# Operations of five attention rounds moved ahead or behind in the order of a hybrid decoder layer

## The chip, the cores and the metric

The kernel runs on one core of a Trainium2 chip. The core's engines are called as in the profile: PE (TensorE, matrix products), ACT (ScalarE), DVE (VectorE), POOL (GpSimd), SP (SyncE, which here issues the weight loads). Each engine works through its own queue of instructions; semaphores hold an instruction until what it reads is there, or until the buffer that it writes is free. The metric is the device time of one execution in microseconds; the time of a kernel is the median of several executions.

## The reference, cut to what matters

The kernel computes one layer of a decoder in float32 for 512 tokens of width 1024. Two token mixers run side by side on the normalised input: NSA, a sparse attention of 8 heads in 2 key/value groups, and GLA, a gated linear attention in chunks. Memory cross-attention and a gated ConvFFN follow. The change touches the NSA part, whose core is

```python
s = s - slopes * dist
p_cmp = masked_softmax(s, dist >= 0)          # compressed keys: 31 of them
o_cmp = jnp.einsum('bhgqn,bnhd->bqhgd', p_cmp, v_cmp)
...
p_slc = masked_softmax(s, mask)               # selected blocks: with 8 blocks of 64, all keys up to the query
o_slc = jnp.einsum('bhgqk,bhqkd->bqhgd', p_slc, vg)
...
p_win = masked_softmax(s, mask)               # the window: at most 256 keys back
o_win = jnp.einsum('bhgqk,bkhd->bqhgd', p_win, vwb)
```

The three results are weighted by sigmoid gates and added.

## The kernel before

**Tiling.** Tokens are cut into four blocks of 128, features into tiles of 128. A float32 operand that must keep its precision is split into a high and a low part: ACT writes the high part (`wh`, `pth`, lines 140 and 165) and DVE the rest (`wl`, `ptl`, lines 141 and 166). A product of two such operands is three matmuls (lines 160 to 162, or 197 to 199). Weights arrive as `raw` tiles from SP's queue and are split on the way.

**Rounds.** The attention runs in eight rounds, one for each key/value group `kv` and token block `i`; round r is `kv*4 + i`. `nsa_scores` forms the scores of four heads in PSUM (PE, lines 581, 597 to 613), adds the mask and takes the row maximum (DVE, lines 583 to 585, 603, 615), exponentiates (ACT, line 631, eight a round, after DVE's `nm` of line 622), sums and takes the reciprocal (DVE, lines 627, 634, 635) and scales the probabilities by the gates (DVE line 639, ACT lines 641 and 643, POOL line 645). `nsa_values` takes the scaled probabilities in pieces of 128 keys: four transposes into a PSUM bank `pt` (PE, line 669), the split into `pth` and `ptl` (ACT, then DVE), and two products into the bank `o` (PE, line 663); at the end ACT and DVE add the two halves (lines 683, 688) and split the result. The loop turn of round r issues first the values of round r-1 (`nsa_values(*prev)`), then the scores of round r (`nsa_scores(kv, i)`), then `fill(...)`: matmuls of other work (`fill_ps_acc`, dense products of the GLA projections), so that PE has something to do. The values of round 7 come last, behind the loop.

**After the rounds** comes the GLA part. `dense_tok` (lines 197 to 199) makes the GLA values: 96 matmuls into four banks (`acc_533`, `acc_534`, `sc_535`, `sc_536`), which nothing holds up but weights and banks, so that the scheduler puts them between the pieces of rounds 5 to 7. Then `gla_att` (line 814), `gla_states` (line 769, 21 matmuls, then a chain of DVE operations, line 781) and further fillers, the first of which is `fill_ps_acc_583`.

**PSUM** has eight banks: two `acc`, three `sc`, two `pt`, one `o`.

**What sets the order.** The code is written round by round, and a scheduler of the framework puts each engine's instructions into a fixed order, by priorities that follow the place in the code; `tc.high_priority(offset=n)` shifts the priority of what is issued inside it by n places, ahead for n > 0 and behind for n < 0. An engine then keeps that order, whatever becomes ready first.

## Time and profile before

| | us |
|---|---|
| time before, median of three runs | 864.42 (863.22 to 865.28) |
| profiled execution, its own time | 862.94 |
| profiled execution, span from the first to the last instruction | 861.1 |
| PE busy in the span | 848.0 (98%) |
| DVE busy | 564.7 (66%) |
| ACT busy | 424.5 (49%) |
| POOL busy | 175.5 (20%) |

Times in views of the trace are microseconds from the start of the span. In a timeline, a row is a run of like instructions of one engine: its start, the time it took, the engine and line, the operation with its output and inputs (buffer numbers left out), the count, and in brackets how long the engine had stood idle before it and for whom. The durations of PE's rows overlap, since matmuls are pipelined; the distance between starts says how fast PE goes.

### The profile page before, as it was taken

The numbers are of one execution on the slowest core, as the hardware profiler recorded it, in microseconds if no ns is written. First come the engines' busy times: TensorE is split into PE (matmuls) and PEld (weight loads), VectorE is DVE, ScalarE is ACT, GpSimd is POOL, SyncE is SP. The second block draws the span as 40 slices with busy tenths as digits, with TensorE's granted clock in tenths as the row PEclk, the third lists the DMA queues.
The fourth block names the chain that finished last, engine by engine and source line by source line (L and its number), as shares of the span: only waits on it lengthen the run. The fifth ranks groups of instructions, "written<-read, shape, count | busy, mean of one in ns | idle before, by whom it ended". The sixth has DMA issues, their size and how long they took to land.

```text
span 861.1 us, 11067 instructions
## 1 busy us (share of the span) xinstructions
PE 848.0 (98%) x4172; PEld 707.6 (82%) x4172; DVE 564.7 (66%) x930; ACT 424.5 (49%) x742; POOL 175.5 (20%) x150
## 2 busy tenths in 40 slices
PE   9999999999999999999999999999999999999997
PEld 6988788777878888898888888888888888888996
DVE  7576998989979667454587759665433455656434
ACT  8466878787444455344455545433311233334321
POOL 2373354412000024203200412111100022121001
PEclk9999999999999999999999999999999999999999
DMA  8332210102221242254331132222222222222402
GB/s 293 120 127 98 74 50 25 49 25 74 74 77 58 86 147 98 97 173 144 127 120 49 56 116 99 99 98 97 98 98 98 98 99 98 97 98 78 143 25 99
DMA packets 26406, 83.58 MB, mean 97 GB/s; under 512 B 3056, under 2 KB 5104, under 8 KB 26352
## 3 DMA queue, kind: packets, MB, share of 16 engines
q1 hardware_dynamic: 26064, 82.58, 27.7%
q8 instruction: 33, 0.54, 0.2%
q10 hardware_dynamic: 288, 0.28, 0.1%
q14 instruction: 21, 0.17, 0.1%
HBM read 80.76 MB, written 2.10 MB: 96 GB/s over the span
## 4 chain that ended last, share of the span: by engine, by line
PE 89%; DVE 5%; ACT 4%; issue 1%; POOL 1%; DMA 0%; DVEq 0%; ACTq 0%; POOLq 0%
PE up_ps_sc L160 4%; PE up_ps_sc L162 4%; PE up_ps_sc L161 4%; PE fill_ps_acc L160 4%; PE fill_ps_acc L161 4%; PE fill_ps_acc L162 3%; PE up_ps_pt L160 3%; PE up_ps_pt L162 3%; PE up_ps_pt L161 3%; PE up_ps_acc L160 3%; PE up_ps_acc L162 3%; PE up_ps_acc L161 3%; PE nsa_ps_o L663 2%; PE nsa_ps_pt L669 2%; PE down_ps_sc L162 2%; PE down_ps_sc L160 2%
## 5 line engine op out<-in xcount | busy, mean ns | idle before, releaser
L1091 POOL TENSOR_TENSOR up_s<-up_s,up_s 128x512 f32<-128x512 f32 x22 | 40.2, 1827 | 253.6 <-ACT up_wh L140 201.8
L140 ACT ACTIVATE up_wh<-up_raw 128x1024 fp32r<-128x1024 f32 x40 | 42.4, 1061 | 56.5 <-PE up_ps_sc L161 29.7
L141 DVE TENSOR_TENSOR up_wl<-up_raw,up_wh 128x1024 fp32r<-128x1024 f32 x40 | 58.2, 1456 | 15.5 <-ACT up_wh L140 15.4
L160 PE MATMUL up_ps_sc<-xo_g,up_wh 128*128 128x512 f32 x124 | 48.3, 389 | 0.0
L162 PE MATMUL up_ps_sc<-xo_g,up_wl 128*128 128x512 f32 x124 | 48.3, 389 | 0.0
L161 PE MATMUL up_ps_sc<-xo_g,up_wh 128*128 128x512 f32 x124 | 48.2, 389 | 0.0
L160 PE MATMUL up_ps_pt<-xo_g,up_wh 128*128 128x512 f32 x104 | 40.5, 389 | 0.0
L162 PE MATMUL up_ps_pt<-xo_g,up_wl 128*128 128x512 f32 x104 | 40.5, 389 | 0.0
L161 PE MATMUL up_ps_pt<-xo_g,up_wh 128*128 128x512 f32 x104 | 40.5, 389 | 0.0
L160 PE MATMUL fill_ps_acc<-in_g,fill_wh 128*128 128x512 f32 x96 | 38.8, 404 | 0.8 <-DVE fill_t L548 0.8
L161 PE MATMUL fill_ps_acc<-in_g,fill_wh 128*128 128x512 f32 x96 | 38.6, 402 | 0.0
L162 PE MATMUL fill_ps_acc<-in_g,fill_wl 128*128 128x512 f32 x96 | 38.2, 398 | 0.0
L631 ACT ACTIVATE nsa_s<-nsa_s,nsa_nm 128x128 f32<-128x128 f32 (+3 forms) x64 | 34.2, 538 | 6.5 <-DVE nsa_nm L622 6.5
L160 PE MATMUL up_ps_acc<-xo_g,up_wh 128*128 128x512 f32 x88 | 34.2, 389 | 0.0
L161 PE MATMUL up_ps_acc<-xo_g,up_wh 128*128 128x512 f32 x88 | 34.2, 389 | 0.0
L162 PE MATMUL up_ps_acc<-xo_g,up_wl 128*128 128x512 f32 x88 | 34.2, 389 | 0.0
L1087 ACT ACTIVATE up_s<-up_s 128x512 f32<-128x512 f32 x22 | 13.8, 632 | 40.9 <-DVE up_s L1085 40.9
L140 ACT ACTIVATE down_wh<-down_raw 128x1024 fp32r<-128x1024 f32 x9 | 9.5, 1061 | 39.4 <-PE down_ps_sc L161 17.5
L165 ACT ACTIVATE nsa_pth<-nsa_ps_pt 128x512 fp32r<-128x512 f32 x38 | 21.9, 594 | 11.0 <-PE nsa_ps_pt L669 10.7
L162 PEld LDWEIGHTS up_ps_sc<-xo_g,up_wl 128*128 128x128 f32 x124 | 23.3, 188 | 4.9
L161 PEld LDWEIGHTS up_ps_sc<-xo_g,up_wh 128*128 128x128 f32 x124 | 23.3, 188 | 4.8
L160 PEld LDWEIGHTS up_ps_sc<-xo_g,up_wh 128*128 128x128 f32 x124 | 23.3, 188 | 4.8
(975 smaller groups left out, 2685.8 us busy)
## 6 DMA issues: line engine op xcount, KB each, us to landing
up_raw<-in_w SPq DMA_DIRECT2D x44, 512.0 KB, 3.2
fill_raw<-in_w SPq DMA_DIRECT2D x20, 512.0 KB, 3.2
down_raw<-in_w SPq DMA_DIRECT2D x18, 512.0 KB, 3.2
proj_raw<-in_w SPq DMA_DIRECT2D x14, 512.0 KB, 4.1
mix_raw<-in_w SPq DMA_DIRECT2D x12, 512.0 KB, 3.2
mkv_raw<-in_w SPq DMA_DIRECT2D x8, 512.0 KB, 3.2
wout_raw<-in_w SPq DMA_DIRECT2D x8, 512.0 KB, 3.4
in_s<-in_xT SPq DMA_DIRECT2D x8, 256.0 KB, 5.6
```

The source lines that it names most:

```text
L140: nc.scalar.activation(wh[:, c], r[:, c], AF.Copy)
L141: lo.tensor_tensor(wl[:, c], r[:, c], wh[:, c].bitcast(F32), op=ALU.subtract)
L160: nc.tensor.matmul(ps, w[0], x[0], start=first, stop=False)
L161: nc.tensor.matmul(ps, w[0], x[1], start=False, stop=False)
L162: nc.tensor.matmul(ps, w[1], x[0], start=False, stop=last)
L165: nc.scalar.activation(h, src, AF.Copy)
L631: nc.scalar.activation(s[:, :w], s[:, :w], AF.Exp, scale=sl, bias=nm[:, c:c + 1], accum_out=sums[:, c:c + 1])
L663: nc.tensor.matmul(po, v, x, start=j == 0 and x is parts[0], stop=j == last and x is parts[-1])
L669: nc.tensor.transpose(pt[:, g * P:(g + 1) * P], srcs[g], C("ident"))
L1087: nc.scalar.activation(cv, cv, AF.Gelu_apprx_tanh)
L1091: nc.gpsimd.tensor_tensor(gm, gm, cv, op=ALU.mult)
```

## The change

A table gives, for a round, the shift of a kind of operation, and a helper `ahead(kind)` opens the shifted priority around it; `now[0]` holds the round. The operations, their shapes, buffers and transfers stay the same.

```diff
+AHEAD = {
+    0: {"hi": 120},
...
+    7: {"exp": -30, "product": -200, "split": -120, "sum": 30},
+}
...
+    now = ["proj"]
+
+    def ahead(kind):
+        n = AHEAD.get(now[0], {}).get(kind, 0)
+        return tc.high_priority(offset=n) if n else nullcontext()
...
-                    nc.scalar.activation(wh[:, c], r[:, c], AF.Copy)
+                    with ahead("hi"):
+                        nc.scalar.activation(wh[:, c], r[:, c], AF.Copy)
...
-                nc.scalar.activation(s[:, :w], s[:, :w], AF.Exp, scale=sl, bias=nm[:, c:c + 1],
-                                     accum_out=sums[:, c:c + 1])
+                with ahead("exp"):
+                    nc.scalar.activation(s[:, :w], s[:, :w], AF.Exp, scale=sl, bias=nm[:, c:c + 1],
+                                         accum_out=sums[:, c:c + 1])
...
         for i in range(4):
+            now[0] = kv * 4 + i
             if prev is not None:
                 nsa_values(*prev)
             prev = nsa_scores(kv, i)
```

The same wrapping is put around the three dense matmuls ("mm", `mm3` in the dense product), the masks ("mask", lines 583 to 585, 603, 615), the scales ("scale", lines 639 to 645), the transposes ("turn", line 669), the split ("split"), the products ("product", line 663) and the final addition ("sum", lines 683, 688). Rounds 1 to 3 have no entry; 4 has `mm` and `sum`, 5 `mask`, `product`, `scale`, `split`, `sum`, 6 `exp`, `scale`, `turn`. Since `now[0]` is set ahead of `nsa_values(*prev)`, the entries of round r for splits, products, transposes and sums act on the values of round r-1; the entry of round 7 holds for the values of round 7 too.

Lines of the changed kernel are numbered higher: 165 is 181 there, 166 is 182, 603 is 622, 615 is 635, 622 is 642, 631 is 652, 639 is 661, 641 is 663, 643 is 665, 663 is 686, 669 is 693, 769 is 798, 802 is 831, 160 to 162 are 176 to 178. In the rows below a tile's name ends in the number of its buffer and its instance. Pieces of round 6's values are `pt_466` to `pt_484`, those of round 7 `pt_509` to `pt_530`; the probabilities of round 6 are `s_448` to `s_462`, of round 7 `s_491` to `s_505`.

DVE, end of round 7's scores and the scaling of round 6. Before:

```order
L635 TENSOR_TENSOR nsa_cf_464_2058<-nsa_cf_464_2058,proj_gate_107_505 128x12
L615 ISA nsa_s_501_2192,nsa_mx_487_2154<-nsa_ps_sc_500_2189,in_cst_1_61 128x384
L615 ISA nsa_mx_487_2154 128x1
L166 TENSOR_TENSOR nsa_g_391_1785<-nsa_t_443_1987,nsa_g_390_1784 128x128
L166 TENSOR_TENSOR nsa_g_393_1787<-nsa_t_443_1987,nsa_g_392_1786 128x128
L639 TENSOR_SCALAR nsa_s_448_2007<-nsa_s_448_2007,nsa_cf_464_2058 128x384
L639 TENSOR_SCALAR nsa_s_452_2017<-nsa_s_452_2017,nsa_cf_464_2058 128x384
L639 TENSOR_SCALAR nsa_s_456_2027<-nsa_s_456_2027,nsa_cf_464_2058 128x384
L603 ISA nsa_s_503_2197,nsa_mx_487_2154<-nsa_ps_sc_502_2194,in_cst_1_61 128x512
L603 ISA nsa_mx_487_2154 128x1
L615 ISA nsa_s_505_2202,nsa_mx_487_2154<-nsa_ps_sc_504_2199,in_cst_1_61 128x384
```

In the changed kernel:

```order
L182 TENSOR_TENSOR nsa_g_393_1787<-nsa_t_443_1987,nsa_g_392_1786 128x128
L647 TENSOR_REDUCE nsa_sums_445_1995<-proj_cm_157_831 128x4
L635 ISA nsa_s_505_2202,nsa_mx_487_2154<-nsa_ps_sc_504_2199,in_cst_1_61 128x384
L635 ISA nsa_mx_487_2154 128x1
L655 RECIPROCAL nsa_cf_464_2058<-nsa_sums_445_1995 128x12
L642 TENSOR_TENSOR nsa_nm_506_2204<-nsa_mx_487_2154,in_cst_1_61 128x12
L831 TENSOR_TENSOR gla_g_558_2466<-fill_g_290_1384,gla_g_558_2466 64x256
L656 TENSOR_TENSOR nsa_cf_464_2058<-nsa_cf_464_2058,proj_gate_107_505 128x12
L831 TENSOR_TENSOR gla_g_559_2470<-fill_g_290_1384,gla_g_559_2470 64x256
L661 TENSOR_SCALAR nsa_s_448_2007<-nsa_s_448_2007,nsa_cf_464_2058 128x384
L661 TENSOR_SCALAR nsa_s_452_2017<-nsa_s_452_2017,nsa_cf_464_2058 128x384
L661 TENSOR_SCALAR nsa_s_456_2027<-nsa_s_456_2027,nsa_cf_464_2058 128x384
```

The masks of round 7's last head (`s_503`, `s_505`), round 7's `nm_506` and two GLA products now stand ahead of the three scales of `s_448`, `s_452` and `s_456`.

ACT, the exponentials of round 7 and the first splits of round 6's values. Before:

```order
L643 ACTIVATE nsa_s_450_2012<-nsa_s_450_2012,nsa_cf_464_2058 128x384
L643 ACTIVATE nsa_s_458_2032<-nsa_s_458_2032,nsa_cf_464_2058 128x384
L641 ACTIVATE nsa_s_460_2037<-nsa_s_460_2037,nsa_cf_464_2058 128x384
L165 ACTIVATE nsa_pth_467_2076<-nsa_ps_pt_466_2071 128x512
L165 ACTIVATE nsa_pth_470_2085<-nsa_ps_pt_469_2080 128x512
L631 ACTIVATE nsa_s_491_2167,nsa_sums_488_2155<-nsa_s_491_2167,nsa_nm_506_2204 128x512
L165 ACTIVATE nsa_pth_473_2096<-nsa_ps_pt_472_2091 128x512
L165 ACTIVATE nsa_pth_476_2107<-nsa_ps_pt_475_2102 128x512
L626 ACTIVATE proj_cm_158_832<-proj_cm_158_832 128x4x31
L631 ACTIVATE nsa_s_493_2172,nsa_sums_488_2155<-nsa_s_493_2172,nsa_nm_506_2204 128x384
```

In the changed kernel, from the second exponential of round 7 on (the first stands five rows higher):

```order
L652 ACTIVATE nsa_s_503_2197,nsa_sums_488_2155<-nsa_s_503_2197,nsa_nm_506_2204 128x512
L652 ACTIVATE nsa_s_505_2202,nsa_sums_488_2155<-nsa_s_505_2202,nsa_nm_506_2204 128x384
L652 ACTIVATE nsa_s_501_2192,nsa_sums_488_2155<-nsa_s_501_2192,nsa_nm_506_2204 128x384
L652 ACTIVATE nsa_s_493_2172,nsa_sums_488_2155<-nsa_s_493_2172,nsa_nm_506_2204 128x384
L652 ACTIVATE nsa_s_497_2182,nsa_sums_488_2155<-nsa_s_497_2182,nsa_nm_506_2204 128x384
L652 ACTIVATE nsa_s_499_2187,nsa_sums_488_2155<-nsa_s_499_2187,nsa_nm_506_2204 128x512
L652 ACTIVATE nsa_s_495_2177,nsa_sums_488_2155<-nsa_s_495_2177,nsa_nm_506_2204 128x512
L181 ACTIVATE nsa_pth_467_2076<-nsa_ps_pt_466_2071 128x512
L181 ACTIVATE nsa_pth_470_2085<-nsa_ps_pt_469_2080 128x512
L665 ACTIVATE nsa_s_493_2172<-nsa_s_493_2172,nsa_cf_507_2218 128x384
L665 ACTIVATE nsa_s_501_2192<-nsa_s_501_2192,nsa_cf_507_2218 128x384
L663 ACTIVATE nsa_s_503_2197<-nsa_s_503_2197,nsa_cf_507_2218 128x512
```

All eight exponentials of round 7 now stand ahead of `pth_467` and `pth_470`, where before one stood behind them and seven stood among the later splits.

PE, the passage from round 7's last product to the GLA states and the first filler after them. Before, the filler `acc_583` begins behind all 21 matmuls of the states:

```order
L663 MATMUL nsa_ps_o_508_2230<-proj_pc_160_834,proj_vcmp_156_826 128x512
L199 MATMUL gla_ps_sc_536_2328<-gla_wh_541_2361,in_g_47_179 128x512
L755 MATMUL gla_ps_pt_563_2487<-in_cst_1_61,fill_g_340_1583 128x128 x4
L814 MATMUL gla_ps_sc_566_2496<-gla_g_558_2466,gla_g_557_2465 128x128 x4
L814 MATMUL gla_ps_sc_566_2496<-gla_g_559_2470,gla_g_557_2465 128x128 x4
L769 MATMUL gla_ps_sc_570_2514<-gla_s_549_2449,gla_t_564_2492 128x256
L769 MATMUL gla_ps_sc_571_2515<-gla_s_549_2449,gla_t_564_2492 128x256
```

In the changed kernel, from the filler's row on `in_g_40` on (its earlier rows stand among the pieces of rounds 6 and 7):

```order
L178 MATMUL fill_ps_acc_583_2573<-in_g_40_164,gla_wl_545_2392 128x512
L176 MATMUL fill_ps_acc_583_2573<-in_g_43_171,gla_wh_544_2391 128x512
L177 MATMUL fill_ps_acc_583_2573<-in_g_44_172,gla_wh_544_2391 128x512
L798 MATMUL gla_ps_sc_570_2514<-gla_s_549_2449,gla_t_564_2492 128x256
L798 MATMUL gla_ps_sc_571_2515<-gla_s_549_2449,gla_t_564_2492 128x256
L798 MATMUL gla_ps_sc_570_2514<-gla_s_550_2450,gla_t_564_2492 128x256
L798 MATMUL gla_ps_sc_571_2515<-gla_s_550_2450,gla_t_564_2492 128x256
L798 MATMUL gla_ps_pt_573_2517<-gla_s_553_2457,gla_t_564_2492 128x256
L798 MATMUL gla_ps_pt_573_2517<-gla_s_554_2458,gla_t_564_2492 128x256
L178 MATMUL fill_ps_acc_583_2573<-in_g_43_171,gla_wl_545_2392 128x512
L798 MATMUL gla_ps_sc_570_2514<-gla_s_549_2449,gla_t_565_2493 128x256
L798 MATMUL gla_ps_sc_571_2515<-gla_s_549_2449,gla_t_565_2493 128x256
```

Filler matmuls now stand ahead of the states, and one between the states that read `gla_t_564` and those that read `gla_t_565`. On PE the order is the same again from the filler's row on `in_g_46` on. The order of SP is the same throughout, 27 lines of POOL's differ.

## Rows read from the trace of the kernel before

**Rows 1.** The page's chain of work that ended last, share by engine.

```profile
PE 89%; DVE 5%; ACT 4%; issue 1%; POOL 1%; DMA 0%; DVEq 0%; ACTq 0%; POOLq 0%
```

**Rows 2.** Busy us (instructions) by window: length, PE, PEld, DVE, ACT, POOL; clock; DMA.

```profile
130.00:183.45 53.45, 52.10 (x270) 41.05 (x268) 47.49 (x144) 44.83 (x124) 22.08 (x27) 1.00 0.11 40
183.45:221.00 37.55, 36.49 (x196) 28.41 (x197) 33.77 (x69) 26.60 (x54) 5.70 (x7) 1.00 0.17 57
221.00:254.00 33.00, 33.00 (x169) 28.06 (x167) 25.75 (x38) 17.22 (x30) 0.00 (x0) 1.00 0.23 80
254.00:262.00 8.00, 7.32 (x36) 5.43 (x35) 6.87 (x11) 3.41 (x5) 1.05 (x2) 0.79 0.19 68
```

**Rows 3.** Timeline of DVE, then of PE, in rounds 0 and 1.

```profile
87.74 1.73 DVE L141 TENSOR_TENSOR fill_wl<-proj_raw,fill_wh 128x1024 fp32r<-128x1024 f32 x1
...
90.49 0.47 PE L597 MATMUL nsa_ps_sc<-in_pair,proj_g 128*128 128x512 f32 x1 [0.23 <-DVE nsa_mx L615]
...
101.69 0.50 PE L663 MATMUL nsa_ps_o<-nsa_ptl,proj_g 128*128 128x512 f32 x1 [0.66 <-DVE nsa_ptl L166]
```

**Rows 4.** Timeline of PE at the first pieces of round 6, then of DVE.

```profile
183.58 0.66 PE L669 MATMUL nsa_ps_pt<-in_cst,nsa_s 128*128 128x128 f32 x4 [0.23 <-DVE nsa_s L639]
...
181.59 1.93 DVE L639 TENSOR_SCALAR nsa_s<-nsa_s,nsa_cf 128x384 f32<-128x384 f32 x3
183.45 0.67 DVE L603 CUSTOM_DVE_ANT_0 nsa_s<-nsa_ps_sc,in_cst 128x512 f32<-128x512 f32 x1
...
186.08 0.94 DVE L802 TENSOR_TENSOR gla_g<-fill_g,gla_g 64x256 fp32r<-64x256 f32 x2
```

**Rows 5.** Timeline of PE, from round 6's pieces to where the orders meet.

```profile
188.83 0.39 PE L197 MATMUL gla_ps_sc<-fill_wh,in_g 128*128 128x512 f32 x1
...
192.26 0.50 PE L663 MATMUL nsa_ps_o<-nsa_ptl,proj_g 128*128 128x512 f32 x1
...
196.04 0.70 PE L669 MATMUL nsa_ps_pt<-in_cst,nsa_s 128*128 128x128 f32 x4
...
198.98 0.50 PE L198 MATMUL gla_ps_acc<-gla_wl,in_g 128*128 128x512 f32 x1
...
211.65 0.61 PE L814 MATMUL gla_ps_sc<-gla_g,gla_g 128*128 128x128 f32 x4
212.63 0.38 PE L769 MATMUL gla_ps_sc<-gla_s,gla_t 64*128 64x256 f32 x1 [0.37 <-ACT gla_t L165]
...
214.95 0.38 PE L769 MATMUL gla_ps_sc<-gla_s,gla_t 64*128 64x256 f32 x1 [0.29 <-DVE gla_t L818]
...
215.85 0.50 PE L160 MATMUL fill_ps_acc<-in_g,gla_wh 128*128 128x512 f32 x1
...
220.53 0.39 PE L162 MATMUL fill_ps_acc<-in_g,gla_wl 128*128 128x512 f32 x1
220.76 0.39 PE L160 MATMUL fill_ps_acc<-in_g,gla_wh 128*128 128x512 f32 x1
```

**Rows 6.** Groups of DVE, then of ACT, 130 to 221 us: busy, mean ns | idle.

```profile
L166 DVE TENSOR_TENSOR nsa_ptl<-nsa_ps_pt,nsa_pth 128x512 fp32r<-128x512 f32 x28 | 18.4, 685 | 2.3 <-ACT nsa_pth L165 2.2
...
L631 ACT ACTIVATE nsa_s<-nsa_s,nsa_nm 128x384 f32<-128x384 f32 (+3 forms) x40 | 22.4, 563 | 2.0 <-DVE nsa_nm L622 2.0
L165 ACT ACTIVATE nsa_pth<-nsa_ps_pt 128x512 fp32r<-128x512 f32 x28 | 16.2, 594 | 6.3 <-PE nsa_ps_pt L669 6.1 <-ACT nsa_s L631 0.2
L631 ACT ACTIVATION_READ_ACCUMULATOR nsa_s<-nsa_s,nsa_nm 128x1 f32 x40 | 7.6, 189 | 0.0
```

**Rows 7.** Timeline of DVE behind the GLA states, then of PE before the slow clock.

```profile
227.08 0.69 DVE L717 TENSOR_TENSOR fill_g<-fill_ps_acc,proj_rstd 128x512 f32<-128x512 f32 x1 [0.87 <-PE fill_ps_acc L162]
...
253.90 1.00 PE L814 MATMUL gla_ps_sc<-gla_g,gla_g 128*128 128x128 f32 x8
254.84 0.38 PE L769 MATMUL gla_ps_sc<-gla_s,gla_t 64*128 64x256 f32 x1
255.78 0.97 PE L769 MATMUL gla_ps_sc<-gla_s,gla_t 64*128 64x256 f32 x11 [0.56 <-DVE gla_t L849]
```

More of the change, by code (lines that the diff above doesn't have):

```diff
@@ L2 @@
 from collections import deque
-from contextlib import ExitStack
+from contextlib import ExitStack, nullcontext
 import concourse.bass as bass
@@ L26 @@
 GLA_FILL = (1, 1, 1, 1, 1, 1, 1)
+AHEAD = {
+    0: {"hi": 120},
+    4: {"mm": -50, "sum": 300},
+    5: {"mask": 200, "product": 50, "scale": -30, "split": 300, "sum": -120},
+    6: {"exp": 30, "scale": 50, "turn": 120},
+    7: {"exp": -30, "product": -200, "split": -120, "sum": 30},
+}
 SM_GAINS = 40
@@ L172, in dense8 @@
             c = slice(k * P, (k + 1) * P)
-            mm3(ps[:, :n], (w[0][:, c], w[1][:, c]), xs[k], k == 0, k == KT - 1)
+            with ahead("mm"):
+                mm3(ps[:, :n], (w[0][:, c], w[1][:, c]), xs[k], k == 0, k == KT - 1)
         return ps
@@ L602, in nsa_scores @@
             s = s_()
-            nc.vector.tensor_tensor_reduce(out=s[:, :n], in0=ps[:, :n], in1=C("slc")[:, 384 - P * i:512],
-                                           op0=ALU.add, op1=ALU.max, scale=1.0, scalar=-3e38,
-                                           accum_out=mx[:, 4 + g:5 + g])
+            with ahead("mask"):
+                nc.vector.tensor_tensor_reduce(out=s[:, :n], in0=ps[:, :n], in1=C("slc")[:, 384 - P * i:512],
+                                               op0=ALU.add, op1=ALU.max, scale=1.0, scalar=-3e38,
+                                               accum_out=mx[:, 4 + g:5 + g])
             ss.append(s)
@@ L614, in nsa_scores @@
             s = s_()
-            nc.vector.tensor_tensor_reduce(out=s[:, :nw], in0=ps[:, :nw], in1=C("win")[:, off:off + nw],
-                                           op0=ALU.add, op1=ALU.max, scale=1.0, scalar=-3e38,
-                                           accum_out=mx[:, 8 + g:9 + g])
+            with ahead("mask"):
+                nc.vector.tensor_tensor_reduce(out=s[:, :nw], in0=ps[:, :nw], in1=C("win")[:, off:off + nw],
+                                               op0=ALU.add, op1=ALU.max, scale=1.0, scalar=-3e38,
+                                               accum_out=mx[:, 8 + g:9 + g])
             sw.append(s)
@@ L661, in product @@
         def product(j, v, *parts):
-            for x in parts:
-                nc.tensor.matmul(po, v, x, start=j == 0 and x is parts[0], stop=j == last and x is parts[-1])
+            with ahead("product"):
+                for x in parts:
+                    nc.tensor.matmul(po, v, x, start=j == 0 and x is parts[0], stop=j == last and x is parts[-1])
         ready = None
@@ L667, in nsa_values @@
             pt = bank("pt")
-            for g in range(4):
-                nc.tensor.transpose(pt[:, g * P:(g + 1) * P], srcs[g], C("ident"))
-            if j < last:
-                h, l = sb([P, T], F32R, "pth", 2), sb([P, T], F32R, "ptl", 2)
-                split(h, l, pt)
-                parts = (h, l)
-            else:
-                x = PC[i % 2]
-                split(x[0:32], x[32:64], pt[0:32])
-                parts = (x,)
+            with ahead("turn"):
+                for g in range(4):
+                    nc.tensor.transpose(pt[:, g * P:(g + 1) * P], srcs[g], C("ident"))
+            with ahead("split"):
+                if j < last:
+                    h, l = sb([P, T], F32R, "pth", 2), sb([P, T], F32R, "ptl", 2)
+                    split(h, l, pt)
+                    parts = (h, l)
+                else:
+                    x = PC[i % 2]
+                    split(x[0:32], x[32:64], pt[0:32])
+                    parts = (x,)
             if ready is not None:
@@ L682, in nsa_values @@
         bot = t_()
-        nc.scalar.activation(bot[0:64], po[64:128], AF.Copy)
+        with ahead("sum"):
+            nc.scalar.activation(bot[0:64], po[64:128], AF.Copy)
         of = t_()[:, 0:2 * P].rearrange("p (a q) -> p a q", a=2)
@@ L686, in nsa_values @@
         bv = bot.rearrange("p (a b q) -> p a b q", a=2, b=2)
-        for b in range(2):
-            nc.vector.tensor_add(of[b * 64:(b + 1) * 64], pv[0:64, :, b, :], bv[0:64, :, b, :])
+        with ahead("sum"):
+            for b in range(2):
+                nc.vector.tensor_add(of[b * 64:(b + 1) * 64], pv[0:64, :, b, :], bv[0:64, :, b, :])
         for a in range(2):
@@ L704, in layer_kernel @@
     stage[0] = "gla"
+    now[0] = "gla"
     fill(99)
@@ L868, in layer_kernel @@
     a0 = gla_att(*qk[0, 0])
+    now[0] = "g0"
     st = gla_states(0, *ks)
     fill(GLA_FILL[0])
+    now[0] = "g1"
     a1 = gla_att(*qk[0, 1])
@@ L873, in layer_kernel @@
     fill(GLA_FILL[1])
+    now[0] = "g2"
     o = gla_out(0, 0, st[0], *a0)
@@ L876, in layer_kernel @@
     fill(GLA_FILL[2])
+    now[0] = "g3"
     gla_norm(*o)
@@ L879, in layer_kernel @@
     fill(GLA_FILL[3])
+    now[0] = "g4"
     gla_norm(*o)
@@ L883, in layer_kernel @@
     fill(GLA_FILL[4])
+    now[0] = "g5"
     a1 = gla_att(*qk[1, 1])
     fill(GLA_FILL[5])
+    now[0] = "g6"
     o = gla_out(1, 0, st[0], *a0)
     fill(GLA_FILL[6])
+    now[0] = "g7"
     gla_norm(*o)
@@ L891, in layer_kernel @@
     gla_norm(*o)
+    now[0] = "rest"
     stage[0] = "mem"
```

24 lines of the change are left out of this document (13 added, 11 removed).

## The prediction

> **What bounds the kernel now.** I read four views, from the coarse to the fine. The chain that ended last is PE for 89% [rows 1]: the kernel is as long as PE's queue takes, and an order can only win the time in which PE stops. So the second view was the timeline of PE, read for distances between starts. Where nothing holds it, a 128x512 matmul starts 0.23 us after the one before (220.53 to 220.76, [rows 5]); what is longer is a stop. In the third, the brackets of that timeline, DVE is named at most stops of the attention rounds [rows 3, 4]. The fourth, busy time by stretch, says why: from 130 to 183.45 us DVE works 47.5 of 53.4 us and ACT 44.8, from there to 221 DVE 33.8 of 37.5 [rows 2]. In the rounds DVE is almost as full as PE, so its order decides when PE gets its operands. From 221 to 254 PE has no idle time at all [rows 2]; nothing is to be won there.
>
> **The change, part by part.** No operation is added or taken away, and no DMA: SP's order is untouched. POOL's 27 moved lines keep their inputs and stand in a queue that is busy 22.1 of 53.4 us [rows 2]; I cost them at nothing, covered by that slack (a POOL scale that came 1 us late would cost PE up to 1 us at its transposes).
>
> *Round 0 (hi).* A weight split, 1.73 us of DVE at 87.74, stood ahead of masks for which PE stopped 0.23 us at 90.49 [rows 3]. It now stands in an earlier hole. But PE's next stop, 0.66 us before 101.69, is for a `ptl` of DVE that hangs on a chain of decay operations which don't move [rows 3]. PE gets there earlier and waits longer. Between 0 and 0.3 us; I take 0.
>
> *The gate at round 6.* Rounds 4 to 6 lose several microseconds on PE before 183.6 us, but how much of that goes is not read stop by stop: what comes last there is one thing. The first pieces of round 6 need the scaled probabilities `s_448`, `s_452`, `s_456`, the scales of DVE end at 183.45, and PE's transposes of the third stand until 183.58 [rows 4]. What PE gains earlier, it waits for here. The change puts more ahead of these scales on DVE: the two masks of round 7's last head (the wider one 0.67 us) and two GLA products (0.94 us), with the small reads beside them some 2.3 us [rows 4]. Against this, DVE had 5.96 us of idle time from 130 to 183.45 (53.45 less 47.49, [rows 2]), spent waiting for PE or ACT while masks that were ready stood behind; the masks of round 5, moved ahead, and the splits of earlier rounds, interleaved otherwise, go into such holes. The bounds: nothing of the idle time is used and the gate opens 2.3 us later, at 185.9; or all of it, and then PE itself sets the gate, by my count of its matmuls some 2.2 us earlier than now. I take the middle, a gate at the same time, 183.6, because walking through DVE's new order with the durations of the trace I find about as much idle time filled as work put ahead.
>
> *What stands behind the gate.* Counted in the two orders from the third scale's transposes to the filler row on which the orders meet, PE has 105 matmuls of 512 columns before and 98 in the changed kernel, and in both 68 transposes or the like and 21 state matmuls. Seven have gone ahead of the gate, into time in which PE waits for it: 7 x 0.227 = 1.59 us. Before, this stretch takes 183.58 to 220.76, 37.18 us [rows 4, 5].
>
> *Stops behind the gate, before.* From 188.83 to 192.26 PE starts 9 matmuls of 512 and 8 transposes, which at 0.227 and 0.117 us (eight small ones from 253.90 to 254.84, [rows 7]) take 2.98 us, and they took 3.43: 0.45 lost. From 196.04 to 198.98 it is 7 and 8, 2.53 against 2.94: 0.41 lost. From 211.65 to 215.85, 25 small ones at 0.117 are 2.93 against 4.20: 1.27 lost, three waits of the states for `gla_t` and its like, two of them 0.37 and 0.29 [rows 5]. Together 2.13 us. In the new order the last goes almost wholly: filler matmuls stand ahead of the states and one among them, and by the time PE has done them the splits of `gla_t` (0.59 on ACT, 0.69 on DVE by their like, [rows 6]) are over.
>
> *Stops behind the gate, new.* ACT has all eight exponentials of round 7 ahead of the first split of round 6, 8 x (0.563 + 0.189) = 6.0 us [rows 6]. What hides this is PE's run of `dense_tok`, 24 matmuls, 5.4 us, between the transposes and the first product that needs `pth_467`; they were spread over the pieces before. My walk has the split done about 1 us before PE asks. If the cover is gone, PE waits for what is missing, one for one. The pieces themselves then follow closely, 13 of them with two `pt` banks. A bank is held for four transposes (0.47), a split on ACT (0.594) and one on DVE (0.685) [rows 6, 7], 1.75 us and hand-offs, with two banks about 0.9 to 1.0 us a piece; PE's own work there, transposes, two products and filler, is about 1.0. So that is even on paper, with half a microsecond here and there: 0.9 us in all, bounds 0 and 4.
>
> [...]
>
> *The sum.* Gate 0, moved matmuls -1.59, stops -2.13 + 0.9 = -1.23: **-2.8 us**. Other small hand-off losses stay as they are.
>
> *Behind the meeting point.* The chain of DVE operations on the states ends hardly earlier than before, since DVE had no slack; but behind it DVE waits 0.87 us for PE at 227.08 [rows 7] and is idle 7.3 of the 33 us to 254 [rows 2], so it can catch up 2.8 us before PE next needs it closely, at 255.78 [rows 7]. There the order is the old one and PE stops as before. I take nothing lost; bounds 0 and 2.8.
>
> The profiled execution took 862.94 us, 1.5 below the median of the three times; its span is 861.1 and what lies around it, 1.8, doesn't change. 862.94 - 2.8 = 860.1 on its footing, 864.42 - 2.8 = **861.6** on the median's.
>
> **The rivals.**
> *A. Given back.* DVE is the second bound: the gate opens up to 2.3 us later, or the state chain, no earlier than before, holds PE behind the meeting point. For it speaks DVE's 33.8 of 37.5 us [rows 2]; against it the idle 7.3 us to 254. Left is 0 to 1.5 us of gain: about 863.7, from 862.9 to 865.
> *B. The pieces bunch, slower.* The exponentials come late or a piece takes 1.4 us instead of 1.0, because ACT and DVE also carry the weight splits and evacuations between the pieces. Then 13 x 0.4 = 5.2 us are lost against 2.8 won: 866.8. It decides from 0.22 us more a piece on. For it: ACT waited 6.1 us for transposes and DVE 2.2 for ACT in these splits [rows 6]; against it, 28 splits of 0.685 us are only 18.4 of DVE's time.
> [...]
> *D. More of the same.* The gate opens 2 us earlier, set by PE itself: 859.6.
>
> **How the numbers follow.** Forecast 0.55 (its own range 860.2 to 862.6), A 0.2, B 0.1, C spared 0.04 and doubled 0.03, D 0.08. A measurement of this kernel can tell about 0.2%, 1.7 us, from no change: faster means below 862.7, slower above 866.1. Faster: the forecast, C spared and D, 0.67, and the early edge of the rest, 0.03: 0.70. Slower: most of B and a tail of A, 0.11. The same: 0.19. The range leaves out B and the far ends of A and D: 858.5 to 865.0.
>
> **What would show it.** In the changed kernel's trace the third scale of round 6 on DVE should end near 183.5 us, the filler row on `in_g_46` should start near 218.0 instead of 220.76, the waits of the states for `gla_t` should be under 0.3 us together, and ACT should have `pth_467` done before PE's wait. The DVE row of 227.08 should start 2 to 3 us earlier with a similar or smaller wait. I am wrong if the gate lies beyond 185, if transposes of rounds 6 and 7 stand more than 1.2 us apart on the mean, or if PE gets idle time between 221 and 254.

## The result, and the profile after

The changed kernel took 859.29 us (median of 859.0 to 860.6), the kernel before 864.46 beside it on the same chip: a ratio of 0.9944, with an interval of 0.9927 to 0.9962, or 5.2 us less. The forecast was 2.8 us less. The profiled executions differ by 3.7 us (862.94 and 859.21). These three numbers are not the same thing, and most of what follows is about why.

Of the lines that the views below name and that have not been paired yet, 243 is 260 in the changed kernel, 634 is 655, 635 is 656, 717 is 746, 781 is 810, 814 is 843, 818 is 847 and 849 is 878.

The windows of after, with the bounds of [rows 2] (columns as there):

```profile
130.00:183.45 53.45, 52.31 (x278) 42.53 (x276) 48.42 (x150) 44.85 (x125) 21.84 (x26) 1.00 0.12 40
183.45:221.00 37.55, 36.37 (x201) 28.94 (x200) 31.53 (x58) 27.93 (x55) 7.74 (x8) 1.00 0.16 57
221.00:254.00 33.00, 32.44 (x176) 27.64 (x175) 28.86 (x47) 17.96 (x31) 0.00 (x0) 1.00 0.23 80
254.00:262.00 8.00, 7.88 (x37) 5.76 (x36) 7.50 (x10) 1.98 (x5) 1.05 (x2) 1.00 0.21 68
```

Two things stand out against [rows 2]. Up to 183.45 us PE has done 278 matmuls where it had done 270, in the same time; DVE has 0.9 us more work there and 2.2 us less behind. And the last window has a granted clock of 1.00 where before it was 0.79.

The gate, which answers to [rows 4], on DVE and on PE:

```profile
182.50 1.06 DVE L661 TENSOR_SCALAR nsa_s<-nsa_s,nsa_cf 128x384 f32<-128x384 f32 x3
183.59 1.36 DVE L832 CAST gla_g<-gla_g 64x512 fp32r<-64x512 f32 x2
...
183.08 1.19 PE L693 MATMUL nsa_ps_pt<-in_cst,nsa_s 128*128 128x128 f32 x8
```

The last scale of DVE ends at 183.56 (183.52 before), and PE does its eight transposes in one piece, with less than 0.1 us lost before any of them, where before it had lost 0.2 to 0.4 us at each pair. What PE gains in these rounds it loses ahead of the gate, at one mask of DVE:

```profile
173.48 0.44 PE L631 MATMUL nsa_ps_sc<-in_pair,proj_g 128*128 128x384 f32 x1 [0.87 <-DVE nsa_mx L635]
```

The filler row forecast for 218.0 stands further below.

Behind the gate, what is new, on PE, DVE and ACT:

```profile
189.69 0.50 PE L686 MATMUL nsa_ps_o<-nsa_pth,proj_g 128*128 128x512 f32 x1
190.03 0.89 PE L843 MATMUL gla_ps_sc<-gla_g,gla_g 128*128 128x128 f32 x7
192.04 0.66 PE L693 MATMUL nsa_ps_pt<-in_cst,nsa_s 128*128 128x128 f32 x4 [1.12 <-DVE nsa_ptl L182]
...
189.05 0.23 DVE L655 RECIPROCAL nsa_cf<-nsa_sums 128x12 f32<-128x12 f32 x1 [1.49 <-ACT nsa_s L652]
...
189.52 1.87 DVE L661 TENSOR_SCALAR nsa_s<-nsa_s,nsa_cf 128x512 f32<-128x512 f32 x3
191.32 1.27 DVE L182 TENSOR_TENSOR nsa_ptl<-nsa_ps_pt,nsa_pth 128x512 fp32r<-128x512 f32 x2
...
189.04 1.09 ACT L181 ACTIVATE nsa_pth<-nsa_ps_pt 128x512 fp32r<-128x512 f32 x2
```

ACT's eight exponentials are over at 189.0, its two splits follow, and PE's first product starts at 189.69, 0.05 us after the first split ends: the run of `dense_tok` covers the exponentials, with nothing to spare. The stop comes one step later. The second halves of the splits, `ptl_468` and `ptl_471`, stand on DVE behind the three scales of round 7, and PE waits 1.12 us for them (1.29 by the distance of its starts).

The states and the row where the orders meet, which answer to the second half of [rows 5]:

```profile
215.63 0.40 PE L798 MATMUL gla_ps_pt<-gla_s,gla_t 64*128 64x256 f32 x2
215.96 0.49 PE L178 MATMUL fill_ps_acc<-in_g,gla_wl 128*128 128x512 f32 x1
216.38 0.74 PE L798 MATMUL gla_ps_sc<-gla_s,gla_t 64*128 64x256 f32 x8
216.97 0.28 PE L798 MATMUL gla_ps_pt<-gla_s,gla_t 64*128 64x256 f32 x1
217.30 0.97 PE L798 MATMUL gla_ps_sc<-gla_s,gla_t 64*128 64x256 f32 x6
218.20 0.50 PE L176 MATMUL fill_ps_acc<-in_g,gla_wh 128*128 128x512 f32 x1
```

The last line is the filler row on `in_g_46`, at 218.20 instead of 220.76. From a few rows later to 255 us every row of PE is 2.42 us earlier than before; it was already 0.07 earlier at 86.8, in a part that nothing touched, so the order gives **2.35 us**. Behind 258 us the rows are 3.9 us earlier: 1.5 us more, where before the lower clock stood. The groups of [rows 6] did not change (splits of DVE 684 ns on the mean, of ACT 594, exponentials 563). For [rows 7], DVE's row of 227.08 starts at 225.63 without a wait, 1.45 us earlier where 2 to 3 had been forecast.

**What the stops add up to.** I took the distance of each two starts of PE, subtracted what such a matmul takes where nothing holds it (by the medians of both traces 0.227 us for 512 columns, 0.109 for 128, others by their width), and summed what is left from 0.1 us on; how the other widths are set moves a sum by some 0.2 us. "Ahead" is from the scores of `nsa_ps_sc_320` at 121 us to the transposes of the third scale, "behind" from there to the meeting row. The rows of the single parts belong to the experiments.

| kernel | ahead: matmuls, us, stops | behind: matmuls, us, stops |
|---|---|---|
| before | 320, 62.60, 4.5 | 194, 37.18, 3.3 |
| after | 328, 62.69, 2.6 | 186, 34.59, 2.4 |
| rounds 4 to 6 alone | 328, 62.71, 2.5 | 186, 36.35, 4.1 |
| round 7 alone | 320, 62.56, 4.5 | 194, 36.44, 2.6 |
| without products set back | 328, 62.69, 2.7 | 186, 35.11, 3.3 |
| without splits set back | 328, 62.63, 2.5 | 186, 34.73, 2.0 |

**What the clock adds.** Each execution reports its span and its mean granted clock. Those of the kernel before fall on three steps: 859.8 us at 0.998 or 0.999, 861.3 at 0.996 or 0.997, 862.9 at 0.994 or 0.995, that is none, one or two stretches at the lower clock, of some 1.6 us of loss each (a single execution, of 863.1 us, reports 0.944 and is counted with the last). The changed kernel falls on the same steps from 857.4 up. Over all runs, with the experiments told of below (the first comparison's four executions of the kernel before are not in the table, since only their times are known):

| kernel | executions with none, one, two | span with none |
|---|---|---|
| before | 31, 33, 29 | 859.8 |
| after | 3, 1, 0 | 857.4 |
| after without round 0 | 7, 3, 1 | 857.7 |
| round 0 alone | 1, 3, 8 | 859.6 |
| rounds 4 to 6 alone | 3, 6, 3 | 858.9 |
| round 7 alone | 8, 2, 1 | 859.2 |
| fillers ahead of the second states | 8, 3, 0 | 860.9 |
| scales set back | 6, 0, 0 | 856.9 |
| evacuation ahead | 7, 3, 2 | 857.6 |
| both of these | 7, 3, 2 | 856.7 |
| row sums set back | 2, 8, 2 | 859.6 |
| the same on the order of before | 0, 4, 2 | none seen |
| without products set back | 7, 0, 0 | 858.0 |
| without splits set back | 3, 3, 0 | 857.6 |

Four executions far longer than the rest (937, 1708 twice and 4823 us) are left out, and the profile of the fillers ahead of the second states, taken in the first of them at a clock of 0.848, is used only for who waits for whom.

### The profile page after: what moved, and what is told of

Same layout as the page of the kernel before. It is cut to its first block, busy times and chain, and to the rows that moved or that the text cites. A ratio compares the mean times of both kernels' runs of the same rounds, so it can differ in the third digit from the quotient of the medians.

```text
span 857.4 us, 11083 instructions
## 1 busy us (share of the span) xinstructions
PE 844.4 (98%) x4172; PEld 706.7 (82%) x4172; DVE 563.6 (66%) x930; ACT 424.0 (49%) x742; POOL 176.1 (21%) x150
## 4 chain that ended last, share of the span: by engine, by line
PE 88%; DVE 6%; ACT 4%; issue 1%; POOL 1%; DVEq 0%; ACTq 0%; POOLq 0%
PE up_ps_sc L177 4%; PE up_ps_sc L176 4%; PE up_ps_sc L178 4%; PE fill_ps_acc L176 4%; PE fill_ps_acc L177 4%; PE fill_ps_acc L178 3%; PE up_ps_pt L177 3%; PE up_ps_pt L176 3%; PE up_ps_pt L178 3%; PE up_ps_acc L177 3%; PE up_ps_acc L176 3%; PE up_ps_acc L178 3%; PE down_ps_sc L178 2%; PE nsa_ps_pt L693 2%; PE down_ps_sc L177 2%; PE down_ps_sc L176 2%
## 5 line engine op out<-in xcount | busy, mean ns | idle before, releaser
L652 ACT ACTIVATE nsa_s<-nsa_s,nsa_nm 128x384 f32<-128x384 f32 (+3 forms) x64 | 34.3, 538 | 5.7 <-DVE nsa_nm L642 5.6
L182 DVE TENSOR_TENSOR nsa_ptl<-nsa_ps_pt,nsa_pth 128x512 fp32r<-128x512 f32 x38 | 25.2, 685 | 4.4 <-ACT nsa_pth L181 3.8
L176 PEld LDWEIGHTS up_ps_sc<-xo_g,up_wh 128*128 128x128 f32 x124 | 23.3, 188 | 4.9
```

What stands on the lines that cost most here:

```text
L176: nc.tensor.matmul(ps, w[0], x[0], start=first, stop=False)
L182: nc.vector.tensor_sub(l, src, h.bitcast(F32))
L652: nc.scalar.activation(s[:, :w], s[:, :w], AF.Exp, scale=sl, bias=nm[:, c:c + 1], accum_out=sums[:, c:c + 1])
```

## The experiments

**Round 0 alone.**

```diff
     0: {"hi": 120},
-    4: {"mm": -50, "sum": 300},
-    5: {"mask": 200, "product": 50, "scale": -30, "split": 300, "sum": -120},
-    6: {"exp": 30, "scale": 50, "turn": 120},
-    7: {"exp": -30, "product": -200, "split": -120, "sum": 30},
```

> Only the row of round 0 ("hi": 120) stands in the table; everything else is in the order of the kernel before. Theory: the stop of 0.45 us that goes near 90 us is taken back at 100.4 and 105.1 us, where a ptl of DVE hangs on decay operations that did not move; by 118.3 us PE stands within 0.1 us of the kernel before and the time differs by less than 0.5 us. Rival: the stop is won for good, -0.45 us, and PE's rows stay that much earlier at 118.3 us.

Measured: 1.001 (0.9997 to 1.0022) of the kernel before; with no stretch 859.6 us, in a single execution, against 859.8. In the trace the rows of PE were 0.30 us later than before at 86.9, by the start of the span, and 0.31 later at 121: nothing won, as forecast. This execution had two stretches at the lower clock, and so shows the second place, which the profile of before had not shown. Its windows (columns as in [rows 2]), PE's timeline at the first group of states, and last a window of the kernel before:

```profile
211.00:215.00 4.00, 3.23 (x27) 2.50 (x25) 3.93 (x9) 3.05 (x6) 0.00 (x0) 1.00 0.00 0
215.00:219.00 4.00, 3.90 (x13) 3.18 (x14) 3.81 (x11) 0.72 (x2) 0.00 (x0) 0.57 0.36 113
219.00:255.00 36.00, 36.00 (x181) 30.50 (x180) 26.99 (x43) 17.73 (x30) 0.00 (x0) 1.00 0.22 76
255.00:259.90 4.90, 4.22 (x29) 3.07 (x27) 4.90 (x9) 2.84 (x4) 0.08 (x1) 1.00 0.07 15
259.90:263.30 3.40, 3.40 (x10) 2.62 (x9) 2.41 (x4) 0.69 (x1) 0.97 (x2) 0.50 0.36 137
...
212.78 0.38 PE L798 MATMUL gla_ps_sc<-gla_s,gla_t 64*128 64x256 f32 x1 [0.40 <-ACT gla_t L181]
...
215.09 0.38 PE L798 MATMUL gla_ps_sc<-gla_s,gla_t 64*128 64x256 f32 x1 [0.28 <-DVE gla_t L847]
...
215.00:219.00 4.00, 4.00 (x21) 3.31 (x22) 3.81 (x10) 0.71 (x2) 0.00 (x0) 1.00 0.36 132
```

The clock falls to its lower level (0.50 of the full one) right behind the first group of states and again behind the second, each time after some 4 or 5 us in which PE was busy for 0.7 us less than the window. The first and the fourth window hold the stops, the second and the fifth the lower clock. In the trace of the kernel before, the same first group with the same waits (0.37 and 0.29 us, [rows 5]) brought no fall: its clock from 215 to 219 us is 1.00. Nor was the number of stretches that of the kernel before: 19 in 12 executions, where that kernel has 0.98 an execution over all, 0.7 to 1.2 by chip.

**Rounds 4 to 6 alone, and round 7 alone.**

The first kernel:

```diff
-    0: {"hi": 120},
...
-    7: {"exp": -30, "product": -200, "split": -120, "sum": 30},
```

The second:

```diff
-    0: {"hi": 120},
-    4: {"mm": -50, "sum": 300},
-    5: {"mask": 200, "product": 50, "scale": -30, "split": 300, "sum": -120},
-    6: {"exp": 30, "scale": 50, "turn": 120},
```

> Only the rows of rounds 4, 5 and 6. Theory: this part carries the seven matmuls of dense_tok that go ahead of the gate of round 6; the gate itself stays near 183.6 us and the pieces behind it keep the old order, so PE is 1.6 us earlier at round 7's pieces and at the filler row where the orders meet again (219.2 instead of 220.76). Time -1.6 us, apart from what the granted clock does at 254 to 262 us. Rival: rounds 4 to 6 fill idle time that the old order of round 7 gives back, because DVE is the bound: 0 us at the meeting row and in the time.

> Only the row of round 7. Theory: the stretch up to the gate is the old one, and behind it the three groups of stops (0.45, 0.41 and 1.27 us) go, against 0.9 to 1.5 us of new stops where products wait for splits: -0.6 to -1.2 us at the meeting row, adding up with rounds 4 to 6 to the whole change's -2.4. Rival: the parts do not add up; without the matmuls moved ahead the exponentials of round 7 delay the splits with nothing to cover them, and this part alone is 0 to 3 us slower.

Measured: 0.9989 (0.9977 to 1.0) and 0.9977 (0.9967 to 0.9986). At the meeting row PE was 0.7 us earlier with rounds 4 to 6, 0.8 with round 7 (less the offset that the rows already have at 87 us, by the start of the span), and the spans with no stretch are 0.9 and 0.6 below that of before. So the size forecast for round 7 held (0.6 to 1.2), that for rounds 4 to 6 did not (1.6), and the parts do not add up: they give 1.5 us and the whole 2.35 (2.5 at the meeting row itself). The table of stops says how. Rounds 4 to 6 do move eight matmuls ahead of the gate and save 2.0 us of stops there, with the gate unmoved; but behind it the stops rise from 3.3 to 4.1. On DVE of that kernel:

```profile
193.47 0.23 DVE L655 RECIPROCAL nsa_cf<-nsa_sums 128x12 f32<-128x12 f32 x1 [0.61 <-ACT nsa_s L652]
193.73 0.17 DVE L656 TENSOR_TENSOR nsa_cf<-nsa_cf,proj_gate 128x12 f32<-128x12 f32 x1
193.94 1.21 DVE L661 TENSOR_SCALAR nsa_s<-nsa_s,nsa_cf 128x512 f32<-128x512 f32 x2
```

and of the kernel before:

```profile
195.04 1.88 DVE L639 TENSOR_SCALAR nsa_s<-nsa_s,nsa_cf 128x512 f32<-128x512 f32 x3
```

Round 7's scales wait for ACT's last exponential, which in the old order of round 7 stands among the splits, and start at 193.94, only 1.1 us earlier than before (195.04); in the changed kernel they start at 189.52. So I read it that the second bound, ACT and DVE together, takes half of the gain back; no run moved these scales alone on this order. The two parts are worth more together than singly.

**Fillers ahead of the second states,** on the order of before: the table holds this row alone.

```diff
+    "g4": {"mm": 120},
```

> All attention rounds in the order of the kernel before; only behind them 24 filler matmuls (acc_662, key g4) stand ahead of the second group of GLA states, which at 254.84 us waited 0.83 us for a PSUM bank and behind it 0.38 and 0.20 us. Theory on the clock: the stretch at the lower granted clock (258.0 to 261.4 us) follows these stops; with them gone it goes too, the granted clock of the whole is 0.999 in all executions and the time is 1.4 + 1.6 = 3.0 us shorter. Rival 1: the stretch falls from execution to execution whatever the order is, so only 1.4 us go and the clock is sometimes 0.997. Rival 2: the stops come back at the next need of the same bank, 0 us.

Measured: 0.9997 (0.9987 to 1.0007); with no stretch 860.9 us, 1.1 longer than before, and never two stretches. PE's timeline behind these states shows who waits now:

```profile
284.73 0.49 PE L176 MATMUL fill_ps_acc<-nsa_g,fill_wh 128*128 128x512 f32 x1 [1.47 <-DVE fill_g L746]
```

The stops at the states are gone, and in their place PE waits behind them for a PSUM bank that DVE has not evacuated (copied out). So rival 2 held for the order (the wait comes back, and costs 1.1 us more than it saved), and the clock was better than in the kernel before, though not always at the full level.

**The change without round 0.**

```diff
-    0: {"hi": 120},
```

> The whole change without its row of round 0. Theory: that row is worth nothing, and the change is two things: 2.3 us of order (PE's rows behind the meeting point 2.3 us earlier, where both kernels run at the full granted clock: shortest span 857.3 against 859.6) and fewer stretches at the lower granted clock, each worth 1.7 us. So the shortest spans here are 857.2 to 857.5, the spans fall on steps of 1.7 us above it, and the mean lies below that of the kernel before by 2.3 plus 1.7 times the difference in stretches per execution. Rival 1: the whole 5.2 us of the first comparison belong to the order, and the ratio is 0.994 on every chip. Rival 2: round 0 carries 0.45 us, shortest span 857.8.

Measured: 0.9964 (0.9951 to 0.9978), a mean of 860.1 us against 863.1. With no stretch 857.7 us (857.3 to 858.0), against 857.4 for the whole change on another chip: no more than the spread. The theory held, in both halves. At equal clock the order is worth 2.1 to 2.4 us, and the rest is that stretches fall in 4 of 11 executions where the kernel before has them in 62 of 93. The 5.2 us of the first comparison are in part luck: by their times the four executions of before that stood beside it had one or two stretches each.

**The scales of round 7 set back.**

```diff
-    7: {"exp": -30, "product": -200, "split": -120, "sum": 30},
+    7: {"exp": -30, "product": -200, "split": -120, "sum": 30, "scale": -60},
```

> The change with round 7's scales set back by 60, so that on DVE the splits ptl_468 and ptl_471 stand behind the first of the three scales and not behind all. Theory: the new stop of 1.29 us that PE has at 190.64 (transposes of pt_472 wait for ptl_468) is DVE's queue; two scales of 0.63 us less ahead of it take it to nearly nothing, and PE is 0.8 to 1.3 us earlier at the filler row in_g_46 (217.1 instead of 218.2) and in the time. Rival: DVE's tail behind the pieces is the second bound, what is won at 190 is lost by 218, 0 us.

Measured: 0.9956 (0.9939 to 0.9972). DVE and PE at the place of the new stop:

```profile
189.86 0.49 DVE L661 TENSOR_SCALAR nsa_s<-nsa_s,nsa_cf 128x512 f32<-128x512 f32 x1
190.26 1.28 DVE L182 TENSOR_TENSOR nsa_ptl<-nsa_ps_pt,nsa_pth 128x512 fp32r<-128x512 f32 x2
191.46 1.36 DVE L661 TENSOR_SCALAR nsa_s<-nsa_s,nsa_cf 128x512 f32<-128x512 f32 x2
...
191.00 0.66 PE L693 MATMUL nsa_ps_pt<-in_cst,nsa_s 128*128 128x128 f32 x4
```

With two of DVE's scales behind the splits and not ahead, PE's transposes start at 191.00 with 0.24 us lost instead of 1.29. At 249 us, where the order is again that of the change, PE is 3.04 us ahead of the kernel before instead of 2.35 (starts taken off): 0.7 of the 1.05 us are kept, the rest goes into small stops at 193 and 201 us (0.34 and 0.22). The cause of the stop is shown; the forecast of 0.8 to 1.3 was a little high. Of the spans with no stretch, 0.5 to 0.8 us are left (856.9), and of the times 0.2 to 0.5, since this build spends 2.1 us outside the span and not 1.8. By the median of its times it is the fastest order found, by little.

**The evacuation ahead, and both edits.**

```diff
-    7: {"exp": -30, "product": -200, "split": -120, "sum": 30},
+    7: {"exp": -30, "product": -200, "split": -120, "sum": 30}, "g3": {"evac": 40},
...
-            nc.vector.tensor_add(pu, ps[:, 0], pu)
+            with ahead("evac"): nc.vector.tensor_add(pu, ps[:, 0], pu)
```

The second kernel has `"scale": -60` in round 7 as well.

> The change, and one DVE row more: the second evacuation of gla_out (gla_ps_sc_635) goes ahead of the 0.69 us product L890. It frees the PSUM bank that the second group of states waits for at 252.42 us. Theory: the stop of 0.83 us shrinks to 0.2 and the rest of that group stays, -0.6 us behind 256 us. On the clock: if the lower clock behind 255 us follows these stops, its stretch gets rarer still. Rival: the 0.38 and 0.20 us stops behind it grow by as much, 0 us.

> Both of the two edits before on the change. Theory: they stand at places 60 us apart and add up, -1.4 to -1.9 us against the change, shortest span 855.4 to 855.9, the fastest of all orders here. Rival: DVE gives one of them back, -0.6 us.

Measured: 0.997 (0.9956 to 0.9983) and 0.9964 (0.9951 to 0.9978); with no stretch 857.6 and 856.7, so the evacuation brings nothing and the rival holds. PE with the evacuation ahead:

```profile
252.72 1.20 PE L798 MATMUL gla_ps_sc<-gla_s,gla_t 64*128 64x256 f32 x11
254.85 0.49 PE L260 MATMUL gla_ps_pt<-gla_sqh,in_ones 128*128 128x512 f32 x1 [0.93 <-ACT gla_sqh L181]
```

The stop of 0.83 us shrinks to 0.22 as forecast. But the scheduler now sets the sum of rows L260 ahead of the filler, and PE waits there, 1.08 us instead of 0.38 and the rest. Nor did the lower clock get rarer: 7 stretches in 12 executions in each of the two kernels, where the change with its scales set back, on the same chip, had none in 6. The profiled execution of both edits met the lower clock behind this stop, and for twice the usual time (6.8 us):

```profile
250.00:254.00 4.00, 3.29 (x25) 2.64 (x23) 4.00 (x6) 2.66 (x4) 0.00 (x0) 1.00 0.00 0
254.40:261.20 6.80, 6.80 (x17) 5.06 (x17) 5.02 (x6) 0.69 (x1) 1.05 (x2) 0.50 0.25 80
```

**The row sums set back,** with the evacuation ahead as well and the filler's matmuls a little ahead, first on the change with the scales set back, then on the order of before. The table of the second kernel:

```diff
+    "g3": {"evac": 40},
+    "g4": {"rows": -50, "mm": 20},
...
-        sum_rows(pn, *hl)
+        with ahead("rows"): sum_rows(pn, *hl)
```

> The change with the scales of round 7 set back as before, and the second group of GLA states freed of its stops in another way: the second evacuation ahead on DVE, and the two sums of rows (L260, L261) that waited for gla_sqh, with the three states behind them, moved back behind the 24 matmuls of the filler acc_662. Theory: of the stops of 0.83, 0.38 and 0.20 us at 252 to 255 us 0.2 are left, -1.2 us against the scales alone; shortest span 855.5 to 855.8 against 856.7. On the clock: with the stops at both groups of states gone the lower clock appears there in almost no execution. Rival 1: the six states of gla_ps_sc_651, now behind 13 fillers instead of 24, wait for their PSUM bank about as long, 0 us. Rival 2 on the clock: it falls as often as in the change (one stretch in two executions), whatever PE does there.

> All attention rounds in the order of the kernel before (the table empty for them), and only the second group of states freed of its stops in the way of the run before. The first group keeps its 1.27 us of stops at 211 to 215 us. Theory: -1.2 us at the full clock (shortest span 858.3 against 859.5), and of the two places at which the lower clock appeared (215 and 258 us) only the first is left: at most one stretch of 1.7 us in an execution, never two. Rival: as often two as in the kernel before (four executions in ten).

Measured: 1.0004 (0.9993 to 1.0015) and 1.0041 (1.0025 to 1.0058): the first, by its spans with no stretch, 2.7 us slower than with the scales alone, the second, by its ratio, 3.5 slower than the kernel before. All theories on the time fell, and those on the clock with them: of the second kernel two executions in six had two stretches, where never two were forecast. In the second kernel PE, DVE and the windows:

```profile
274.34 0.50 PE L176 MATMUL fill_ps_acc<-nsa_g,fill_wh 128*128 128x512 f32 x1 [2.86 <-DVE fill_g L746]
...
266.40 3.35 DVE L245 RECIPROCAL gla_t<-gla_t 128x512 f32<-128x512 f32 x1
...
271.76 1.23 DVE L157 TENSOR_TENSOR fill_wl<-fill_raw,fill_wh 128x1024 fp32r<-128x1024 f32 x1
272.90 0.68 DVE L182 TENSOR_TENSOR gla_g<-gla_t,gla_g 128x512 fp32r<-128x512 f32 x1
273.60 1.29 DVE L746 TENSOR_TENSOR fill_g<-fill_ps_acc,proj_rstd 128x512 f32<-128x512 f32 x2
...
271.00:274.50 3.50, 0.64 (x6) 0.50 (x6) 3.42 (x7) 3.46 (x8) 0.00 (x0) 1.00 0.14 29
275.00:278.50 3.50, 3.50 (x10) 2.77 (x9) 3.41 (x6) 1.57 (x3) 0.00 (x0) 0.51 0.18 70
```

Moving the sums behind the filler moves the reciprocal of 3.35 us on DVE with them, ahead of the evacuations (L746) that free the filler's banks, and PE stops for 3.0 us. On the clock this is the clearest pair of runs, though not in the way it was meant: of the 18 executions of the two kernels 16 had a stretch at the lower level (of the first kernel 10 in 12, where the scales alone had none in 6), and in both traces it stands right behind the stop, at 271.6 and at 275.1 us, and no longer at 258.

**Without the products set back, and without the splits set back.**

```diff
-    7: {"exp": -30, "product": -200, "split": -120, "sum": 30},
+    7: {"exp": -30, "split": -120, "sum": 30},
```

```diff
-    7: {"exp": -30, "product": -200, "split": -120, "sum": 30},
+    7: {"exp": -30, "product": -200, "sum": 30},
```

> The change without the entry that sets round 6's and 7's products back (product -200 of round 7). All eight exponentials still stand ahead of pth_467, and the run of dense_tok ahead of the first product; but from there on each product follows right behind its split, with no matmul of dense_tok or filler between. Theory: PE has no cover for a split's 0.6 + 0.7 us and stops at most products, some 0.3 us at each of a dozen: 2 to 4 us are lost, the order's gain of 2.3 us is gone. Rival: the pieces follow DVE's and ACT's pace in either order, and the time stays within 0.5 us of the change.

> The change without the entry that sets round 6's splits back (split -120 of round 7): on ACT pth_467 and pth_470 stand ahead of round 7's eight exponentials again, pth_473 among them; on DVE ptl_468, 471 and 474 stand ahead of round 7's scales. Theory: this entry is what keeps the gain of rounds 4 to 6. With the splits first, ACT's last exponential ends 1.8 us later than in the change (three splits of 0.6 us), DVE's scales and the pieces of round 7 follow it, and of the 2.3 us 0.7 to 1.0 are left, as with rounds 4 to 6 alone. Rival: the exponentials have room in either order, since dense_tok stands between; only the stop of 1.29 us at 190.64 goes, and the time is 0.8 to 1.3 us below the change.

Measured: 0.9966 (0.9952 to 0.998) and 0.9957 (0.9944 to 0.9971); with no stretch 858.0 and 857.6. Both theories fell. Products right behind their splits cost 0.5 us at the meeting row, 0.4 behind it, and not 2 to 4: the rival held, the pieces go at the pace of ACT and DVE in either order, and the stops behind the gate rise by 0.9 us. Splits ahead of the exponentials cost nothing at all (2.4 us won behind the meeting row, as in the change), and bring none of the 0.8 to 1.3 us of the rival: the stop of 1.29 goes, one of 0.60 at 185.8 and some small ones come. The last exponential of ACT starts at 190.10 instead of 188.22, and that is early enough for the scales (ACT, then DVE):

```profile
190.10 0.72 ACT L652 ACTIVATE nsa_s<-nsa_s,nsa_nm 128x512 f32<-128x512 f32 x1
...
191.41 0.49 DVE L661 TENSOR_SCALAR nsa_s<-nsa_s,nsa_cf 128x512 f32<-128x512 f32 x1
```

So neither entry by itself is what makes the two parts add up. Which of the rest (the exponentials, the sums, or any two of the four together) does it was not tried.

## Why the prediction came out as it did

**The gate, forecast at 183.6, no change: right in time, in part by another wait.** It takes 62.69 us from the row at 121 where it took 62.60, and the third scale ends where it did (183.56). But PE no longer stands there for DVE's scales: it comes to them with less than 0.1 us to wait, since it has lost its time ahead, 1.03 us behind 172.22 for a mask of DVE. That PE is held by DVE up to here is as forecast; that PE would come to the gate at the same moment by another of DVE's waits was not argued, and is in part luck.

**Seven matmuls ahead of the gate, -1.59: right in size.** The trace shows eight more, one of them small; the stops ahead of the gate fall by 1.9 us. But as an argument the step is incomplete: it took for granted that what is won ahead of the gate stays won behind it. Rounds 4 to 6 alone keep 0.7 of it. It was the new order of round 7 that let it through.

**Stops behind the gate, -2.13 + 0.9: measured -0.9 instead of -1.2.** The old stops went nearly as forecast; of the states' 1.27 us 0.41 are left (0.20 and 0.21 beside the two fillers), where I had said less than 0.3. The new ones were mis-sized and put on the wrong engine. I had costed ACT, where the exponentials were indeed covered by `dense_tok` (PE's product starts at 189.69; the split ends 0.05 us earlier, where 1 us was forecast), and not DVE, where the three scales that hang on these exponentials stand ahead of `ptl_468`. That is one stop of 1.29 us; setting two of the scales back gave 0.7 us. A split of DVE whose input was there at 189.64 ran at 191.32, behind 1.87 us of scales. ACT shows the same: the transposes that feed its first split ran from 183.08 us on, all eight were over at 184.27, and the split started at 189.04, behind the exponentials.

**Pieces of about 1.0 us: right where the pieces follow each other.** Round 7's last five sets of transposes start 0.95 to 1.2 us apart (207.23 to 211.46). By its letter the sign of being wrong, more than 1.2 us apart on the mean, is met: the 13 sets from 192.04 to 211.46 stand 1.62 us apart. It was a bad sign, since other matmuls stand between them and PE loses little there; before, the mean from 185.88 on was 1.86.

**Behind the meeting point nothing lost: right, by a narrow margin.** DVE's chain on the states was not "hardly earlier" but 2 us later than before, and was level again only at 240 us; PE did not wait for it. The 0.56 us that PE is idle between 221 and 254, which by its letter is a sign of being wrong too, is the old stop at the second states, which ended at 255.78 and now falls into the window:

```profile
253.36 0.97 PE L798 MATMUL gla_ps_sc<-gla_s,gla_t 64*128 64x256 f32 x11 [0.56 <-DVE gla_t L878]
```

**Round 0, 0: right,** by its own run.

**The clock: the step that failed.** The sum of the order, -2.8, stands against -2.35 measured. Taken off the median of before, 864.46, that is 862.1, close to the forecast of 861.6; the 859.29 measured lies below the forecast's own range of 860.2 to 862.6. What the times show beyond the order is fewer stretches at the lower clock, "C spared" in the chances, to which I gave 0.04. I had read the clock off one execution as if it belonged to the kernel: one stretch of 1.7 us (8 us at 0.79 on the mean, [rows 2]), there or not. In fact the order of before has two places for it (215 us, by the run with round 0 alone, and 258), each taken in some executions only, one stretch per execution on the mean; the change, with and without round 0, has 6 in 15 executions, 0.4. That is 0.6 x 1.6 = 1.0 us on the mean, about a third of what the change brings. In the first comparison 2.8 us are left beyond the order, since its executions of the kernel before, by their times, had one or two stretches each: some 1.8 us of that number were luck.

What makes the stretch rarer is shown in part. Between 100 and 300 us it stands behind stops of PE wherever a trace has it (215, 254, 256, 258, 260, 272, 275 us), moves with them, and came in 16 of the 18 executions of the two kernels with a stop of 3 us. Thinning the first group of states goes with fewer stretches (after, round 7 alone). But the second group kept its stops of 0.83, 0.38 and 0.20 us in the change, in the run with the scales set back and in the one without the products, and the last two had no stretch in 13 executions, while the kernel before has one there or at the first group in two of three. And round 0 alone, with the stops of before, had more stretches than the kernel before. So the stops are not the whole cause, and why the same stops bring the lower clock in one order or execution and not in another stays open. One rival is untested: no run kept the stops and moved only the time at which they fall.

## What to carry to other kernels

Where two engines are almost full, an order that helps one round is worth what the next round lets through (here 0.7 and 0.8 us for the parts alone, 2.5 for the whole at the meeting row): cost the parts together, and walk both queues behind a gate, the one that releases it and the one that hangs on it. Before a difference of a few tenths of a per cent is explained, look at the granted clock of every execution (here 0.998 or 0.999 against 0.994 or 0.995 went with 3.1 us of span), and compare spans at the same clock. A stop that is taken out by moving one operation is not gone before the operations that hang on it have found a place as well: three of four such repairs here came back as another wait.
